# A hybrid diffusion step on one core: the backward recurrence's operands in two tiles with slots of their own, and q's low half over fixed zeros

## The chip, the cores and the metric

The kernel runs on one core of one Trainium2 chip. The metric is the device time of one execution in microseconds (us), as the median of several. The engines are TensorE (PE, with its weight load PEld), VectorE (DVE), ScalarE (ACT), GpSimd (POOL) and SyncE (SP). Nearly all transfers between HBM and the on-chip memory are issued by SP, in program order, on one queue.

## The reference, cut to what matters

One layer of a trunk: 128 context tokens and 2048 latent tokens on a grid 64 wide, 1024 channels, all in float32. After a normalisation one product gives q, k, v for 8 heads of 64 channels, and the two inputs of a recurrence over 512 channels. Each latent token attends to an 8 by 16 neighbourhood and to 128 cached context keys; the recurrence runs forward and backward over the tokens:

```python
s_loc = jnp.einsum('bqhd,bkhd->bhqk', qr, kb).astype(jnp.float32) * ATT_SCALE + bias
...
hf = rg_lru(xc, lru_a[0], lru_wr[0], lru_br[0], lru_wi[0], lru_bi[0], h0[:, 0], False)
hb = rg_lru(xc, lru_a[1], lru_wr[1], lru_br[1], lru_wi[1], lru_bi[1], h0[:, 1], True)
out = (hf + hb).astype(yb.dtype) * jax.nn.gelu(yb)
```

Attention and `out` go side by side through one output projection, then come a gated residual, a second normalisation, a SwiGLU feed-forward part and a last normalisation.

## The kernel before

To keep float32 accuracy on PE, an operand x is split into a high part and a low part (x minus the high part), and a product is made of several products of parts. The kernel runs in phases: 1 makes q, k, v and the forward recurrence and writes them to scratch in HBM (`qs`, `ks`, `vs`, `lrs`); 2 is attention together with the backward recurrence; 3a is the output projection; 4 and 5 are the feed-forward part. The order of instructions is written out by hand and each engine works through its own list in order.

**Phase 2, attention.** Heads go in four pairs p. The latent grid is cut into 16 blocks of 128 queries, four row blocks rb by four column blocks cb; a fifth row block, rb 4, holds the context tokens. So there are 4 times 17 = 68 blocks, and each has one unit for each of the two heads: 136 units. For the unit at hand `scores` multiplies q by the keys on PE (L913 to L917), and DVE adds the bias (L921); one unit later `probs` takes the exponential (ACT, DVE, POOL); four units later the probabilities are transposed and multiplied by v.

**q and k.** A key tile of a head holds the high half of k in partitions 0 to 63 and its low half in 64 to 127 (`load_keys`, four transfers of 576 KB a pair). `load_rows` loads q of a pair and row block so that the high half of q stands in both halves of the partitions, and the low half of q too: one tile [128, 4, 512], filled by four transfers of 256 KB, each into 64 partitions (L841). Two products with 128 rows of contraction then sum all four products of parts. The tiles of row blocks 0 to 3 share three slots; rb 4 has a tile of its own, `qc`. `load_rows` also loads the values `vg`. The loads are issued two row blocks ahead; at the start of rb 1 come the next pair's bias tables `tz`, keys `k` and context values `vc`.

**The backward recurrence.** `backward` walks through 20 pieces: for each of the four channel groups m four pieces of 512 tokens and one of 128, from the end to the start. For a piece one transfer (L765) fills a tile `bk` [128, 4, 512] with the decay a, the input b, the forward result hf and the gate gl; there are three slots. DVE scans a and b (L780), adds b to hf (L785), multiplies by gl (L788), and SP stores hf to `mix` (L89). It is a generator that is resumed at every second unit, once a block: a piece of 512 takes three blocks, one of 128 takes one. The load of piece i + 2 is issued one block after the scan of piece i:

```python
            nc.vector.tensor_copy((self.st[:, 4 + m:5 + m] if s0 == 0 else self.bstate[:, m:m + 1]), b[:, 0:1])
            if s0:
                yield
            load(i + 2)
            nc.vector.tensor_add(hf, hf, b)
```

Its slot is that of piece i - 1, whose last reader is the store of hf. A store is put on a list and issued at the start of the next unit.

**SP.** SP's list holds loads and stores in program order, and an instruction that waits holds all behind it. Each transfer counts up one of eight completion counters, DMAHW0 to DMAHW7 in turn, and waits until the transfer eight places before it has landed; so at most eight are in flight.

Of the kernel before, what the change touches and what calls it, by code (L numbers as in the profile page):

```python
# [6 lines left out]
F32 = mybir.dt.float32  # L7
F32R = mybir.dt.float32r
BF16 = mybir.dt.bfloat16
AF = mybir.ActivationFunctionType  # L10
OP = mybir.AluOpType
# [36 lines left out]
def f32(ap):  # L48
    return ap.bitcast(F32)
# [16 lines left out]
class Body:  # L66
# [687 lines left out]
    def backward(self, bp):  # L754

        nc = self.nc
        seq = [(m, s0, n) for m in range(4)
               for s0, n in ((1664, 512), (1152, 512), (640, 512), (128, 512), (0, 128))]
        T = {}

        def load(i):
            if i < len(seq):
                m, s0, n = seq[i]
                T[i] = bp.tile([128, 4, 512], F32, name="bk", bufs=3)
                nc.sync.dma_start(T[i][:, :, :n], self.lrs[m, :, :, s0:s0 + n])  # L765

        for i in range(2):
            load(i)
            yield
            yield  # L770
        for i, (m, s0, n) in enumerate(seq):
            t = T.pop(i)
            a, b, hf, gl = (t[:, j, :n] for j in range(4))
            if s0 == 0:
                init = 0.0
            elif s0 == 1664:
                init = self.prm[:, P_ST + 4 + m:P_ST + 5 + m]
            else:
                init = self.bstate[:, m:m + 1]
            nc.vector.tensor_tensor_scan(b[:, ::-1], a[:, ::-1], b[:, ::-1], initial=init, op0=OP.mult, op1=OP.add)  # L780
            nc.vector.tensor_copy((self.st[:, 4 + m:5 + m] if s0 == 0 else self.bstate[:, m:m + 1]), b[:, 0:1])
            if s0:
                yield
            load(i + 2)
            nc.vector.tensor_add(hf, hf, b)  # L785
            if s0:
                yield
            nc.vector.tensor_mul(hf, hf, gl)  # L788
            self.store(self.mix[4 + m, :, s0:s0 + n], hf)
            yield  # L790
# [17 lines left out]

    def att_more(self):
        self.te = self.pool("attb", side="right")  # L810
        self.load_rows(0, 0)
        self.load_bias(0)
        self.load_rows(0, 1)
# [18 lines left out]
    def load_rows(self, p, rb):  # L832

        nc, tp = self.nc, self.te
        ctx = rb == 4
        c0, nq = 512 * rb, 128 if ctx else 512
        q = self.Q[p, rb] = tp.tile([128, 4, nq], F32R, name="qc" if ctx else "q", bufs=1 if ctx else 3)
        for h in range(2):
            src = f32(self.qs[p, :, 64 * h:64 * h + 64, c0:c0 + nq]).rearrange("z f n -> f z n")
            for i in range(2):  # L840
                nc.sync.dma_start(f32(q[64 * i:64 * i + 64, 2 * h:2 * h + 2]), src)  # L841
        if not ctx:
            row0, nr = ROWS[rb][:2]
            for G in range(row0 // 4, (row0 + nr) // 4):
                if (p, G) not in self.V:
                    v = self.V[p, G] = tp.tile([128, 4, 128], F32, name="vg", bufs=8)
                    vd = self.vs[:, G, :, 128 * p:128 * p + 128].rearrange("w k d -> k w d")
                    nc.sync.dma_start(v[:, 1:3], vd[:, 1:3])
                    nc.sync.dma_start(v[:96, 0:4:3], vd[:96, 0:4:3])

    def phase2(self):
        nc, A = self.nc, self.A
        self.ps = self.pool("psum2", space=PSUM)
        tp = self.pool("attw", side="right")
        self.wop = self.pool("wo")
        self.wo = {}
        bp = self.pool("bk")
        K, TZ, Q, V, MO, BT = self.K, self.TZ, self.Q, self.V, {}, {}
# [13 lines left out]
        def bias(blk, h):  # L872

            p, rb, cb = blk
            if rb == 4:
                return bts[0]
            row0, nr, I0, rt = ROWS[rb]
            col0, wc, J0, ct = COLS[cb]
            key = (p, rt, ct, h)
            if key not in BT:  # L880
                BT[key] = bts[nbt[0] % 4]
                nbt[0] += 1
                mo = MOFF[rt, ct]
                nc.gpsimd.tensor_add(
                    BT[key][:, 512 - nr * wc:512].rearrange("p (i j) -> p i j", i=nr),
                    TZ[p, h][:, I0:I0 + nr, J0:J0 + wc],
                    msk[:, mo:mo + nr * wc].rearrange("p (i j) -> p i j", i=nr))
            return BT[key]

        def geom(blk):  # L890
            p, rb, cb = blk
            if rb == 4:
                return 512, 0, 128
            nr, wc = ROWS[rb][1], COLS[cb][1]
            return 512 - nr * wc, nr // 4, 4 * wc
# [3 lines left out]
        def scores(u):  # L899
            blk, h = u  # L900
            p, rb, cb = blk
            off = geom(blk)[0]
            bt = bias(blk, h)
            kt = K[p, h]
            qs = slice(128 * cb, 128 * cb + 128)

            q, r = (Q[p, rb][:, 2 * h + z, qs] for z in range(2))
            S = self.b2()
            if off < 512:
                row0, nr = ROWS[rb][:2]  # L910
                col0, wc = COLS[cb][:2]
                kw = kt[:, 0:2048].rearrange("p (r c) -> p r c", c=64)[:, row0:row0 + nr, col0:col0 + wc]
                nc.tensor.matmul(S[:, off:512], q, kw, start=True, stop=False)  # L913
                nc.tensor.matmul(S[:, off:512], r, kw, start=False, stop=True)
            kc = kt[:, 2176:2304] if rb == 4 else kt[:, 2048:2176]
            nc.tensor.matmul(S[:, 512:640], q, kc, start=True, stop=False)
            nc.tensor.matmul(S[:, 512:640], r, kc, start=False, stop=True)  # L917
            P[u] = tp.tile([128, 640], F32, name="pt", bufs=5)
            SM[u] = tp.tile([128, 4], F32, name="sm", bufs=7)

            nc.vector.tensor_tensor_reduce(out=P[u][:, off:640], in0=S[:, off:640], in1=bt[:, off:640],  # L921
                                           scale=-1.0, scalar=3.0e38, op0=OP.add, op1=OP.min,
                                           accum_out=SM[u][:, 0:1])
# [56 lines left out]
        def rest():  # L980
            yield from self.backward(bp)
            nc.sync.dma_start(A["st"], self.st)
            yield
            ks, raw = (4, 5, 6, 7, 0), {}
            for i in range(len(ks) + 1):
                if i < len(ks):
                    raw[i] = bp.tile([128, 4, 512], F32, name="bk", bufs=3)[:, 0:2].rearrange("p a b -> p (a b)")
                    nc.sync.dma_start(raw[i], A["w_out"][128 * ks[i]:128 * ks[i] + 128, :])
                if i:
                    self.split_wo(self.wop, raw.pop(i - 1), ks[i - 1])  # L990
                yield

        rest = rest()
        units = [(b, h) for b in blocks for h in range(2)]
        nu = len(units)
        LA = 4
        done, opened = None, False
        for i in range(nu + LA + 1):
# [4 lines left out]
            if i < nu:  # L1003
                (p, rb, cb), h = units[i]
                if h == 0 and cb == 0:
                    if rb == 0:
                        self.load_rows(p, 2)
                    elif rb == 1:
                        self.load_rows(p, 3)
                        if p < 3:  # L1010
                            self.load_bias(p + 1)
                            self.load_keys(p + 1)
                            self.load_values(p + 1)
                    elif rb == 3:
                        self.load_rows(p, 4)
                        if p < 3:
                            self.load_rows(p + 1, 0)
                    elif rb == 4 and p < 3:
                        self.load_rows(p + 1, 1)
                scores(units[i])  # L1020
# [13 lines left out]
            if i % 2 and not opened:  # L1034
                try:
                    next(rest)
                except StopIteration:
                    bp.release()
                    self.opened()
                    opened = True  # L1040
# [594 lines left out]
```

## Time and profile before

| | us |
|---|---|
| median of 3 runs (2618.84 to 2628.18) | 2619.93 |
| the profiled execution's own time | 2630.12 |
| its span, first to last instruction | 2628.3 |
| PE busy in the span | 2485.7 (95%) |
| DVE, POOL, ACT busy | 1545.8, 1422.5, 991.5 |
| phase 2, about | 638 to 935 us of the span |

A stretch of the trace has the busy time of each engine with the number of its instructions, then three columns: TensorE's granted clock as a share of full speed, the mean busy share of the 16 DMA engines, and GB/s moved. A wait is put down to the instruction that came last. "SPq" is SP's transfer queue; its durations are those of issuing a transfer, not of moving the data. All times in a timeline count from the span's start.

### The profile page before, as it was taken

The numbers are of one execution on the slowest core, as the hardware profiler recorded it, in microseconds if no ns is written. First come the engines' busy times: TensorE is split into PE (matmuls) and PEld (weight loads), VectorE is DVE, ScalarE is ACT, GpSimd is POOL, SyncE is SP. The second block draws the span as 40 slices with busy tenths as digits, with TensorE's granted clock in tenths as the row PEclk, the third lists the DMA queues.
The fourth block names the chain that finished last, engine by engine and source line by source line (L and its number), as shares of the span: only waits on it lengthen the run. The fifth ranks groups of instructions, "written<-read, shape, count | busy, mean of one in ns | idle before, by whom it ended". The sixth has DMA issues, their size and how long they took to land. (4 is left out here: it accounts for less than half of the span.)

```text
span 2628.3 us, 37477 instructions
## 1 busy us (share of the span) xinstructions
PE 2485.7 (95%) x13976; PEld 2205.0 (84%) x13976; DVE 1545.8 (59%) x2252; ACT 991.5 (38%) x1696; POOL 1422.5 (54%) x962
## 2 busy tenths in 40 slices
PE   7899999999887999979999999999999999999998
PEld 4888777787776788869999999999999978888887
DVE  5665757673665743477666887888666721123222
ACT  3454455565554632133333444443333310021111
POOL 3444455554555644467766788888666532233121
PEclk8999999999988999989999999999999999999999
DMA  6455767559988755734333243323332463343331
GB/s 254 136 167 209 261 200 260 183 192 249 233 230 228 187 168 181 234 111 145 105 100 105 81 167 101 119 92 104 99 105 89 138 243 131 112 144 121 127 108 65
DMA packets 234086, 412.88 MB, mean 157 GB/s; under 512 B 33705, under 2 KB 125609, under 8 KB 232881
## 3 DMA queue, kind: packets, MB, share of 16 engines
q1 hardware_dynamic: 233904, 410.49, 49.0%
q8 instruction: 111, 1.82, 0.3%
q14 instruction: 71, 0.57, 0.1%
HBM read 300.17 MB, written 119.69 MB: 160 GB/s over the span
## 5 line engine op out<-in xcount | busy, mean ns | idle before, releaser
L116 POOL TENSOR_TENSOR wl<-wr,wh 128x1024 fp32r<-128x1024 f32 (+1 forms) x146 | 303.5, 2079 | 384.7 <-ACT wh L110 109.5
L116 POOL TENSOR_TENSOR wl<-su,wh 128x512 fp32r<-128x512 f32 x263 | 396.0, 1534 | 30.3 <-ACT wh L110 29.8
L1488 POOL TENSOR_TENSOR x<-x,tm 128x1024 f32<-128x1024 f32 x33 | 100.0, 3032 | 337.6 <-DVE tm L1487 334.6
L110 ACT ACTIVATE wh<-su 128x512 fp32r<-128x512 f32 x263 | 160.4, 628 | 274.9 <-DVE su L1263 133.4
L546 PE MATMUL mm<-hh,wh 128*128 128x512 f32 (+2 forms) x640 | 213.8, 367 | 7.4 <-DVE hh L112 6.5
L546 PE MATMUL mm<-hl,wh 128*128 128x512 f32 (+2 forms) x640 | 212.2, 364 | 4.5 <-DVE hl L116 4.5
L546 PE MATMUL mm<-hh,wl 128*128 128x512 f32 (+2 forms) x640 | 211.2, 363 | 1.1 <-POOL wl L116 1.1
L1487 DVE TENSOR_TENSOR tm<-b,g 128x1024 f32<-128x1024 f32 x33 | 40.4, 1224 | 289.0 <-PE b L1477 277.4
L1359 POOL TENSOR_TENSOR ua<-ua,gt 128x384 f32<-128x384 f32 (+3 forms) x99 | 165.0, 1673 | 57.8 <-DVE ua L1339 44.5
L930 POOL TENSOR_SCALAR pt<-pt,sm 128x512 f32<-128x512 f32 (+3 forms) x136 | 113.0, 831 | 119.3 <-DVE sm L929 94.1
L116 DVE TENSOR_TENSOR wl<-wr,wh 128x512 fp32r<-128x512 f32 x131 | 140.1, 1069 | 57.2 <-ACT wh L110 57.2
L1263 DVE TENSOR_TENSOR su<-wr 128x512 f32<-128x512 f32 x66 | 115.4, 1749 | 74.5 <-POOL wl L116 74.5
L1474 PE MATMUL b<-wdl,b0h 128*128 128x512 f32 x374 | 147.7, 395 | 3.0 <-POOL wdl L116 2.3
L1473 PE MATMUL b<-wdh,b0h 128*128 128x512 f32 x374 | 147.2, 393 | 1.3 <-ACT wdh L110 1.3
L110 ACT ACTIVATE wh<-wr 128x512 fp32r<-128x512 f32 (+1 forms) x198 | 120.6, 622 | 68.1 <-PE pp L1318 61.6
L546 PEld LDWEIGHTS mm<-hh,wh 128*128 128x128 f32 x640 | 114.5, 193 | 29.6 <-ACT hh L110 8.6
L1474 PE MATMUL b<-wdl,b1h 128*128 128x512 f32 x352 | 138.7, 394 | 0.0
L1473 PE MATMUL b<-wdh,b1h 128*128 128x512 f32 x352 | 138.4, 393 | 0.0
L112 DVE CAST wh<-wr 128x1024 fp32r<-128x1024 f32 x79 | 60.5, 767 | 124.2 <-PE mm L546 73.5
L546 PEld LDWEIGHTS mm<-hl,wh 128*128 128x128 f32 x640 | 114.1, 193 | 20.7 <-DVE hl L116 6.0
L928 ACT ACTIVATE pt<-pt,sm 128x512 f32<-128x512 f32 (+3 forms) x136 | 95.8, 704 | 84.9 <-DVE sm L921 67.2
L546 PEld LDWEIGHTS mm<-hh,wl 128*128 128x128 f32 x640 | 113.7, 192 | 16.7 <-POOL wl L116 1.4
(315 smaller groups left out, 7479.0 us busy)
## 6 DMA issues: line engine op xcount, KB each, us to landing
wr<-in_win SPq DMA_DIRECT2D x80, 512.0 KB
wr<-in_wg SPq DMA_DIRECT2D x66, 512.0 KB
wr<-in_wu SPq DMA_DIRECT2D x66, 512.0 KB
ar<-act_s SPq DMA_DIRECT2D x15, 1408.0 KB
wm<-in_w_mod SPq DMA_DIRECT2D x40, 512.0 KB
x_s<-x SPq DMA_DIRECT2D x34, 512.0 KB
x<-x_s SPq DMA_DIRECT2D x34, 512.0 KB
act_s<-ua SPq DMA_DIRECT2D x44, 384.0 KB
```

The costliest lines, as they stand in the source:

```text
L110: self.nc.scalar.activation(hi, src, AF.Copy)
L112: self.nc.vector.tensor_copy(hi, src)
L116: e.tensor_sub(lo, src, f32(hi))
L546: nc.tensor.matmul(p[:, :x1 - x0], a[:, s], b[k][:, x0:x1], start=first, stop=last)
L928: nc.scalar.activation(x, x, AF.Exp, bias=sm[:, 0:1], scale=-1.0, accum_out=sm[:, 1:2])
L930: nc.gpsimd.tensor_scalar(x, x, sm[:, 2:3], 0.0, op0=OP.mult, op1=OP.add)
L1263: nc.vector.tensor_sub(t, a11, a21)
L1359: self.nc.gpsimd.tensor_mul(O[i][:, a:b], O[i][:, a:b], G[i][:, a:b])
L1473: nc.tensor.matmul(ps[:, s], ah[:, i], wh[:, s], start=(i == 0), stop=False)
L1474: nc.tensor.matmul(ps[:, s], ah[:, i], wl[:, s], start=False, stop=False)
L1487: nc.vector.tensor_mul(tmp, ps, g2[1 if t == 0 else 0])
L1488: nc.gpsimd.tensor_add(x2, x2, tmp)
```

## The change

**Backward recurrence.** The tile `bk` becomes two: `bk0` [128, 2, 512] for a and b with three slots, and `bk2` [128, 2, 512] for hf and gl with four. A piece is loaded by two transfers of 512 KB in place of one of 1 MB. The load of piece i + 2 is issued ahead of the scan of piece i, one block earlier than before. Its a and b take the slot of piece i - 1 (last reader: the add on DVE), its hf and gl that of piece i - 2 (last reader: that piece's store).

**q.** The high half stays in both halves of the partitions, in a tile `q` [128, 2, 512] with three slots, which rb 4 now shares. The low half goes into one of three fixed tiles `ql` [128, 2, 512], in partitions 0 to 63 alone; partitions 64 to 127 hold zeros, written once by GpSimd at the end of phase 1. The product of the two low halves drops out. A row block's q is three transfers of 256 KB in place of four. PE's instructions keep their number and shapes.

```diff
-                T[i] = bp.tile([128, 4, 512], F32, name="bk", bufs=3)
-                nc.sync.dma_start(T[i][:, :, :n], self.lrs[m, :, :, s0:s0 + n])
+                T[i] = []
+                for j, bufs in ((0, 3), (2, 4)):
+                    t = bp.tile([128, 2, 512], F32, name=f"bk{j}", bufs=bufs)
+                    nc.sync.dma_start(t[:, :, :n], self.lrs[m, :, j:j + 2, s0:s0 + n])
+                    T[i] += [t[:, 0, :n], t[:, 1, :n]]
...
-            t = T.pop(i)
-            a, b, hf, gl = (t[:, j, :n] for j in range(4))
+            a, b, hf, gl = T.pop(i)
+            load(i + 2)
...
             if s0:
                 yield
-            load(i + 2)
             nc.vector.tensor_add(hf, hf, b)
...
         self.te = self.pool("attb", side="right")
+
+        self.ql, self.nql = [self.te.tile([128, 2, 512], F32R, name=f"ql{i}") for i in range(3)], 0
+        for t in self.ql:
+            self.nc.gpsimd.tensor_scalar(t[64:128].rearrange("p a b -> p (a b)"),
+                                         self.ident[64:128, 0:1].to_broadcast([64, 1024]), 0.0, 0.0,
+                                         op0=OP.mult, op1=OP.add)
...
-        q = self.Q[p, rb] = tp.tile([128, 4, nq], F32R, name="qc" if ctx else "q", bufs=1 if ctx else 3)
-        for h in range(2):
-            src = f32(self.qs[p, :, 64 * h:64 * h + 64, c0:c0 + nq]).rearrange("z f n -> f z n")
-            for i in range(2):
-                nc.sync.dma_start(f32(q[64 * i:64 * i + 64, 2 * h:2 * h + 2]), src)
+        q = tp.tile([128, 2, 512], F32R, name="q", bufs=3)[:, :, :nq]
+        r = self.ql[self.nql % 3][:, :, :nq]
+        self.nql += 1
+        self.Q[p, rb] = q, r
+        for z, d in ((0, q[0:64]), (0, q[64:128]), (1, r[0:64])):
+            nc.sync.dma_start(f32(d), f32(self.qs[p, z, :, c0:c0 + nq]).rearrange("(h f) n -> f h n", f=64))
...
-            q, r = (Q[p, rb][:, 2 * h + z, qs] for z in range(2))
+            q, r = (z[:, h, qs] for z in Q[p, rb])
...
-                    raw[i] = bp.tile([128, 4, 512], F32, name="bk", bufs=3)[:, 0:2].rearrange("p a b -> p (a b)")
+                    raw[i] = bp.tile([128, 2, 512], F32, name="bk2", bufs=4).rearrange("p a b -> p (a b)")
```

SP's list where the second pair turns to its row block 1 (the third pair's `tz`, `k0`, `k1` and `vc` are loaded here; the `bk` load is that of piece 8), before:

```order
L841 DMA q_6676<-qs_s_62 64x2x512 x4
L848 DMA vg_6681<-vs_s_65 128x2x128
L849 DMA vg_6681<-vs_s_65 96x2x128
L824 DMA tz_6684<-tz_s_73 128x512
L824 DMA tz_6686<-tz_s_73 128x512
L830 DMA k0_6688<-ks_s_63 64x2304 x2
L830 DMA k1_6691<-ks_s_63 64x2304 x2
L819 DMA vc_6694<-in_cv 128x128
L819 DMA vc_6694<-vctx_s_66 128x128
L765 DMA bk_6743<-lrs_s_67 128x4x512
```

The same place of the list with the change:

```order
L768 DMA bk0_6688<-lrs_s_67 128x2x512
L768 DMA bk2_6690<-lrs_s_67 128x2x512
L851 DMA q_6694<-qs_s_62 64x2x512 x2
L851 DMA ql2_5407<-qs_s_62 64x2x512
L858 DMA vg_6698<-vs_s_65 128x2x128
L859 DMA vg_6698<-vs_s_65 96x2x128
L833 DMA tz_6701<-tz_s_73 128x512
L833 DMA tz_6703<-tz_s_73 128x512
L839 DMA k0_6705<-ks_s_63 64x2304 x2
L839 DMA k1_6708<-ks_s_63 64x2304 x2
L828 DMA vc_6711<-in_cv 128x128
```

The load of piece 8 moved from behind q, the bias tables and the keys to ahead of them, and q has one transfer fewer.

SP's list at the same turn one pair later, with what each transfer waits for (a counter DMAHW is that of an earlier transfer); `bk_7823` is piece 15, and `mix_s_68<-bk_7333` stores piece 12, whose slot it takes, before:

```order
L819 DMA vc_7667<-in_cv 128x128 [waits DMAHW3_49]
L819 DMA vc_7667<-vctx_s_66 128x128 [waits DMAHW4_49]
L89 DMA mix_s_68<-bk_7333 128x512 [waits DMAHW5_49,DVE_49]
L89 DMA mix_s_68<-mo_7625 128x512 [waits DMAHW6_49,DVE_49]
L765 DMA bk_7823<-lrs_s_67 128x4x512 [waits DMAHW7_49,DMAHW5_49]
L89 DMA mix_s_68<-bk_7503 128x512 [waits DMAHW0_49,DVE_49]
```

And with the change, where piece 15 is `bk0_7790` and `bk2_7792`:

```order
L828 DMA vc_7689<-in_cv 128x128 [waits DMAHW4_49]
L828 DMA vc_7689<-vctx_s_66 128x128 [waits DMAHW5_49]
L89 DMA mix_s_68<-bk2_7299 128x512 [waits DMAHW6_49,DVE_49]
L768 DMA bk0_7790<-lrs_s_67 128x2x512 [waits DMAHW7_49]
L768 DMA bk2_7792<-lrs_s_67 128x2x512 [waits DMAHW0_49]
L89 DMA mix_s_68<-mo_7650 128x512 [waits DMAHW1_49,DVE_49]
L89 DMA mix_s_68<-bk2_7462 128x512 [waits DMAHW2_49,DVE_49]
```

The load of piece 15 stands behind the keys in both, but the second wait, for the store of piece 12 that was issued two places ahead of it (DMAHW5), is gone.

GpSimd's list at the end of phase 1 with the change; the `wl` are the low halves of phase 1's last three weight tiles, and `bt0` is phase 2's first bias tile:

```order
L709 TENSOR_TENSOR ig_5268<-ig_5268,xc_5080 128x514
L116 TENSOR_TENSOR wl_5320<-wr_5239,wh_5319 128x1024
L116 TENSOR_TENSOR wl_5361<-wr_5276,wh_5360 128x1024
L817 TENSOR_SCALAR ql0_5405<-ident_76 64x1024
L817 TENSOR_SCALAR ql1_5406<-ident_76 64x1024
L817 TENSOR_SCALAR ql2_5407<-ident_76 64x1024
L116 TENSOR_TENSOR wl_5439<-wr_5323,wh_5438 128x1024
L894 TENSOR_TENSOR bt0_5551<-tz_5424,msk_4542 128x288
```

The three fills are new; they stand ahead of the last weight tile's low half.

## Rows read from the trace of the kernel before

**Rows 1.** The profiled execution, its span.

```profile
core 0: 2628.3 us, clock 0.975
```

**Rows 2.** Busy time by stretch: phase 2; 20 us without a wait.

```profile
core 0: us, PE busy (x) PEld busy (x) DVE busy (x) ACT busy (x) POOL busy (x), PEclk, DMA share, GB/s
640.00:935.00 295.00, 243.91 (x2257) 211.59 (x2259) 195.99 (x660) 168.29 (x410) 174.18 (x207) 0.90 0.84 222
850.00:870.00 20.00, 20.00 (x214) 17.84 (x211) 16.31 (x59) 13.93 (x38) 17.66 (x21) 1.00 0.91 222
```

**Rows 3.** Waits of PE and DVE, 636 to 935 us: total, times, longest (us).

```profile
PE b L913 <- DVE sm L921: 47.0, 13, 14.5
DVE bk L780 <- DMA bk<-lrs_s: 42.8, 9, 15.2
...
PE b L913 <- DMA q<-qs_s: 3.7, 2, 2.3
```

**Rows 4.** Timeline of DVE, three scans, one restart; in brackets: idle before.

```profile
714.44 1.28 DVE L780 TENSOR_TENSOR_SCAN bk<-bk,prm 128x512 f32<-128x512 f32 x1 [5.46 <-DMA bk<-lrs_s]
...
757.88 1.28 DVE L780 TENSOR_TENSOR_SCAN bk<-bk,bstate 128x512 f32<-128x512 f32 x1 [10.43 <-DMA bk<-lrs_s]
...
764.90 0.29 DVE L974 COPY mo<-b 128x128 f32<-128x128 f32 x1 [2.07 <-PE b L966]
...
839.47 1.28 DVE L780 TENSOR_TENSOR_SCAN bk<-bk,prm 128x512 f32<-128x512 f32 x1 [15.22 <-DMA bk<-lrs_s]
```

**Rows 5.** Waits of SP's transfer queue, 620 to 935 us.

```profile
SPq L765 <- DMA mix_s<-bk: 56.7, 10, 9.3
...
SPq L89 <- DMA q<-qs_s: 9.5, 15, 1.2
...
SPq L841 <- PE b L966: 2.7, 4, 1.1
```

**Rows 6.** Timeline of SP's transfer queue: start, duration of the issue (us).

```profile
708.53 0.56 SPq L765 DMA_DIRECT2D bk<-lrs_s  x1
...
729.81 2.58 SPq L841 DMA_DIRECT2D q<-qs_s  x4
...
737.90 3.63 SPq L830 DMA_DIRECT2D k<-ks_s  x4
...
742.92 0.57 SPq L765 DMA_DIRECT2D bk<-lrs_s  x1
...
820.86 0.32 SPq L89 DMA_DIRECT2D mix_s<-bk  x1
...
833.65 0.58 SPq L765 DMA_DIRECT2D bk<-lrs_s  x1
```

**Rows 7.** Busy time by stretch: keys alone in flight; 128-partition transfers.

```profile
747.00:754.00 7.00, 3.40 (x37) 2.83 (x35) 0.45 (x4) 1.65 (x4) 1.68 (x2) 0.88 1.01 214
921.00:925.00 4.00, 4.00 (x46) 3.49 (x41) 2.92 (x14) 3.25 (x9) 3.00 (x6) 1.00 1.06 398
```

**Rows 8.** SP's issue of three 512 KB loads; size and count of q's loads.

```profile
918.64 1.54 SPq L1057 DMA_DIRECT2D x<-in_w_out  x3
...
q<-qs_s SPq DMA_DIRECT2D x64, 256.0 KB
```

**Rows 9.** GpSimd around phase 1's end, its nearest shape, PE in the last block.

```profile
623.22 2.39 POOL L116 TENSOR_TENSOR wl<-wr,wh 128x1024 fp32r<-128x1024 f32 x1 [1.94 <-DVE wh L112]
638.71 1.42 POOL L884 TENSOR_TENSOR bt<-tz,msk 128x288 f32<-128x288 f32 x2 [13.11 <-PE mm L546]
...
L930 POOL TENSOR_SCALAR pt<-pt,sm 128x640 f32<-128x640 f32 x32 | 30.8, 963 | 53.4 <-DVE sm L929 38.6 <-PE b L917 5.6 <-DVE mo L974 5.0
...
637.28 0.39 PE L546 MATMUL mm<-hh,wh 128*128 128x512 f32 x1
637.51 0.39 PE L546 MATMUL mm<-hl,wh 128*128 128x512 f32 x1
```

## The prediction

> **What bounds the kernel now.** The change touches phase 2 and one spot at the end of phase 1, so I first read the stretch of phase 2 by itself [rows 2]. PE is busy for 243.9 of 295 us there, at a mean granted clock of 0.90 (1.00 is the higher level, 2.4 GHz). In 20 us without a stall (850 to 870) PE is busy all the time at clock 1.00 and does 214 of the stretch's 2257 matmuls, that is 6.4 of the 68 blocks: 3.1 us a block. At that pace the stretch would take 211 us; so up to 84 us of it are waits and what they bring. The transfer engines, too, are busy: 0.84 of the stretch, and 0.91 in the 20 us in which PE did not wait.
>
> The waits say whose they are [rows 3]. PE's largest, 47.0 us, is for DVE's bias step (L921). DVE is not slow there: its own largest wait is the backward scan's for its operands, 42.8 us in nine times, the longest 15.2. DVE works in order, so the bias steps behind the scan wait with it, and PE behind them. PE waits for q itself only 3.7 us. The timeline has the three large scan waits: 5.46, 10.43 and 15.22 us [rows 4]; the other six share the remaining 11.7. After the 10.43 the pipeline also has to fill again: DVE stands 2.07 us for PE 6 us later.
>
> Why are the operands late? SP's own waits [rows 5] give 56.7 us to the load of `bk` waiting for the store of an earlier piece, whose slot it takes; SP is held that long, and so is every load and store behind. The timeline of the queue [rows 6] shows two kinds. At 742.92 the load is issued right behind four key transfers (737.90) and the scan starts 15 us later: it stands in line. At 820.86 the store is issued, again behind keys, and only at 833.65 does the load follow it: it waits for the store's landing, and the scan starts at 839.47.
>
> How fast is the line? With keys alone in flight, which go into 64 partitions, it moves 214 GB/s with all engines busy; with loads into 128 partitions 398 GB/s [rows 7]. A transfer of q, 256 KB into 64 partitions, thus takes 1.22 us, a key transfer 2.76 and half a `bk` tile 1.32. The Trainium skill ("SBUF — State Buffer", "Door 1: The DMA port swizzle") says that partitions 0 to 63 reach 8 of 16 ports, half of the bandwidth; the trace agrees, 214 to 398.
>
> **The change, part by part.**
>
> *Piece 8.* Its load moves ahead of q, the bias tables and the keys, where q stood at 729.81 [rows 6]: 13.1 us earlier, which is more than the wait of 10.43. Saved 10.4, and the refill of 2.1 behind it [rows 4].
>
> *Piece 5.* Its load at 708.53 had waited for a store; it now needs none that is recent and goes a block (3.1 us) earlier, with half a tile ahead of the scan instead of a whole one (1.3 less). Saved 5.5; at least 3.
>
> *Piece 15.* Its load stays behind the keys but no longer waits for the store's landing at 833.6. It lies right behind that store in the line: half a tile later, 834.9, less one q transfer that is no longer ahead, 833.7. The scan started at 839.47. Saved 5.8, and 9.4 of the wait stay; 3 to 15 as bounds.
>
> *The other six waits, 11.7 us.* Each load goes a block earlier, has half a tile less (1.3) and mostly a q transfer less (1.2) before the scan can start; the mean wait is 2.0. I take 10 as saved, bounds 7 and 11.7.
>
> *What is late next.* Without the pause at piece 8 the scans of pieces 9 and 10 come while the keys (four at 2.76, 11 us) still move, and their loads stand behind these; piece 10's hf and gl also wait for a store that lies behind the keys. I take 2 us of new waits, between 0 and 5.
>
> *q's transfers.* One of four goes [rows 8]. Of the 16 loads of 1 MB three lie at or before the start of phase 2; 13 transfers at 1.22 and four small ones at 0.31 are 17 us of transfer time. They shorten the line, and what of that reaches a scan is counted above; it isn't added again. As a check: 0.84 of 295 us are 248 us of transfer time, 231 after; in a phase of 263 us that is 0.88, below the 0.91 that the line reached while PE never waited. So the line can carry the forecast.
>
> *SP.* q loses 20 issues, `bk` gains 20; an issue takes 0.56 to 0.65 us [rows 6]. Nothing, as SP's queue has waits to spare once the 56.7 are gone.
>
> *The fills.* Three GpSimd operations of 64 by 1024 ahead of the last weight tile's low half. The nearest row, 128 by 640, takes 963 ns [rows 9], hence 1.5 us each. GpSimd is free from 621.3 (1.94 us idle before 623.22); three fills end at 625.9, the low half at 628.3 instead of 625.6. Its block is the last of phase 1: 24 matmuls 0.23 us apart that end at 638.6, so it starts at about 633.1. Hidden, with 4.8 us of cover; a fill would have to take over 3.1 us to cost anything. PE's products with the zero rows keep their shapes: nothing.
>
> *Sum.* 10.4 + 2.1 + 5.5 + 5.8 + 10 - 2 = 31.8 us. The profiled execution took 2630.1 us, its span 2628.3 [rows 1] and 1.8 around it; it becomes 2598. It lies above all three timed runs, whose median is 2619.9; the same saving there gives 2588. With all low bounds (10.4 + 3 + 3 + 7 - 5, no refill) 18 us are saved, with all high ones (42.8 and two refills) 47: from 2573 to 2602.
>
> **The rivals.** *The line is the bound (2603).* The transfer engines are busy 0.84 of the phase already, and an earlier load only stands longer in it. Then the gain is the transfer time cut, 17 us. For it: at 742.92 the load did stand in line, and stores wait for q transfers, with which they share nothing but the counter [rows 5]. Against it: the 0.88 above.
>
> *Halves cost as much as wholes (2620).* Alone, a load of 1 MB took 5.9 us (708.53 to the scan at 714.44), against 2.6 at 398 GB/s: 3.3 us fixed. If each of the 20 added transfers paid that in the line, 66 us would go; from 1.6 on the gain is used up. Against it: three loads of 512 KB issued within 1.54 us [rows 8] ran at 398 GB/s together [rows 7]. The pieces were loaded two ahead before as well, so that the change might do little is part of this case. The Trainium skill ("DMA: Bandwidth & Descriptors", "Measured") asks for transfers of at least 1 MiB, and its section "Anatomy of one DMA" puts a fixed cost of about 2.0 us on each, measured on GpSimd's path; by that, 20 more would cost an estimated 40 us in the line and the time would be 2628. The 398 GB/s speak against it for transfers in a row.
>
> *The shared ring holds SP (2635, slower).* With rb 4 in q's ring, the first three row blocks of pairs 1 to 3 take a slot that PE has only just left, where before it had been left a block or more earlier: nine loads at which SP may stand for PE, with all stores and `bk` loads behind. To end above 2633 each must keep the line idle for over 5.0 us ((31.8 + 13.1) / 9); at 5.2 the time is 2635. Against it: today's waits of this kind are 2.7 us in four [rows 5], PE needs q ten units (five blocks, 15 us) after the issue, and SP is late rather than early.
>
> **How the numbers follow.** What a measurement can tell here is about 0.5%, 13.1 us. Chances: forecast 0.76; the line 0.13, of which 0.03 would stay within 0.5%; halves 0.07; the ring 0.04. Faster: 0.76 + 0.10 = 0.86; same 0.10; slower 0.04. The range takes in the forecast's bounds but for the last 3 us of the high ones, and the line's 2603 with 3 us to spare: 2576 to 2606.
>
> **What would show it.** DVE's wait at the scan falls from 42.8 to about 13 us, nearly all of it at piece 15; the wait at piece 8 is gone; SP's wait of the `bk` load for a store falls from 56.7 to under 20; phase 2 takes about 263 us with a transfer share of 0.88; phase 1 ends at the same time. I am wrong if DVE still waits over 25 us there, if PE's wait for q grows to over 10, or if the transfer share reaches 1.0 while scans wait at every piece.

## The result and the profile after

The changed kernel takes 2581.7 us (median of four runs, 2573.7 to 2584.1) against 2621.3 for the kernel before (2618.8 to 2628.2 in four): the ratio is 0.984, 95% interval 0.981 to 0.987. That is faster by 39.6 us, or 1.5%. The profiled execution took 2581.9 us, its span 2580.1.

Phase 2 from its first bias step to its last, in the columns of [rows 2]; the first row is of the kernel before, the second of the changed one:

```profile
639.50:931.30 291.80, 240.60 (x2227) 209.07 (x2226) 194.51 (x654) 165.34 (x403) 173.90 (x205) 0.90 0.85 225
636.20:883.30 247.10, 231.90 (x2227) 201.84 (x2227) 195.02 (x654) 165.93 (x403) 179.20 (x204) 0.97 0.93 248
```

The phase is 44.7 us shorter, 247.1 in place of 291.8. PE does 2227 matmuls in both. Its idle time falls from 51.2 to 15.2 us, 36.0 less; the other 8.7 us are that it is busy for a shorter time with as many matmuls, at a mean granted clock of 0.97 in place of 0.90. What comes behind takes 1697.0 and 1696.8 us.

The waits of PE and of DVE after, 636 to 900 us:

```profile
PE b L923 <- DVE sm L931: 11.1, 14, 3.2
PE b L923 <- DMA q<-qs_s: 2.9, 1, 2.9
PE b L924 <- DMA ql<-qs_s: 1.0, 1, 1.0
```

```profile
DVE bk L784 <- DMA bk<-lrs_s: 6.1, 3, 4.2
```

These answer to [rows 3]: the scan's wait for its operands fell from 42.8 to 6.1 us, and PE's wait for the bias step from 47.0 to 11.1. Where the 6.1 are, and what came of piece 8, the scans in DVE's timeline show (start, duration, and in brackets the idle time before):

```profile
678.61 1.28 DVE L784 TENSOR_TENSOR_SCAN bk<-bk,bstate 128x512 f32<-128x512 f32 x1 [4.18 <-DMA bk<-lrs_s]
...
733.65 1.27 DVE L784 TENSOR_TENSOR_SCAN bk<-bk,bstate 128x512 f32<-128x512 f32 x1
744.11 0.41 DVE L784 TENSOR_TENSOR_SCAN bk<-bk 128x128 f32<-128x128 f32 x1
747.86 1.27 DVE L784 TENSOR_TENSOR_SCAN bk<-bk,prm 128x512 f32<-128x512 f32 x1
757.05 1.83 DVE L784 TENSOR_TENSOR_SCAN bk<-bk,bstate 128x512 f32<-128x512 f32 x1 [0.67 <-DMA bk<-lrs_s]
...
800.56 1.73 DVE L784 TENSOR_TENSOR_SCAN bk<-bk,prm 128x512 f32<-128x512 f32 x1 [1.20 <-DMA bk<-lrs_s]
```

The rows are pieces 2, 8, 9, 10, 11 and 15 (counted from 0). Pieces 8, 9 and 10 wait for nothing; of the 15.22 us at piece 15 [rows 4] 1.20 are left. The longest wait is now at piece 2, which stands behind the keys of the second pair; it was 3.15 us before and has grown.

SP's waits, 620 to 900 us, answer to [rows 5]:

```profile
SPq L89 <- DVE mo L984: 20.9, 8, 10.8
SPq L768 <- DMA k<-ks_s: 16.2, 7, 2.8
...
SPq L851 <- PE b L950: 8.9, 1, 8.9
SPq L768 <- DMA mix_s<-bk: 6.2, 5, 2.4
```

The `bk` load's wait for a store fell from 56.7 to 6.2 us. What holds that load most now are the keys ahead of it in the line, 16.2 us. The 20.9 us are stores that wait for DVE's results, 19.4 of them after 840 us, when no `bk` load is left to come.

GpSimd around the end of phase 1, with the three fills:

```profile
615.64 2.40 POOL L116 TENSOR_TENSOR wl<-wr,wh 128x1024 fp32r<-128x1024 f32 x1 [3.92 <-issue]
618.13 3.65 POOL L817 TENSOR_SCALAR ql<-ident 64x1024 fp32r<-64x1024 f32 x3
621.86 2.40 POOL L116 TENSOR_TENSOR wl<-wr,wh 128x1024 fp32r<-128x1024 f32 x1
```

They take 3.65 us together and stand behind a low half that ends at 618.0; the last low half ends at 624.3, before the 625.6 of [rows 9].

The span fell by 48.2 us, more than the median, because the one profiled execution of the kernel before lies 8.8 us above its median and that of the changed kernel at its own. 3.3 of the 48.2 are the earlier end of phase 1, which lies between 635.5 and 639.5 us in the thirteen profiles of this study, with and without the change.

### The profile page after: what moved, and what is told of

Its sections match the earlier page's. It is cut to its first block, busy times and chain, and to the rows that moved or that the text cites. A ratio compares the mean times of both kernels' runs of the same rounds, so it can differ in the third digit from the quotient of the medians.

```text
span 2580.1 us, 37465 instructions
## 1 busy us (share of the span) xinstructions
PE 2474.4 (96%) x13976; PEld 2195.5 (85%) x13976; DVE 1545.4 (60%) x2252; ACT 992.0 (38%) x1696; POOL 1432.5 (56%) x965
## 5 line engine op out<-in xcount | busy, mean ns | idle before, releaser
L1487 PE MATMUL b<-wdh,b0l 128*128 128x512 f32 x374 | 116.6, 393 | 0.0
```

Source lines behind the costliest of these rows:

```text
L1487: nc.tensor.matmul(ps[:, s], al[:, i], wh[:, s], start=False, stop=(i == 10))
```

## The experiments

Unless a diff says otherwise it is against the changed kernel. Scan waits, SP waits and the length of phase 2 (first bias step to last) are of each kernel's one profile, times are medians. The kernel before was timed again beside them, with medians of 2621.1 to 2623.2 us.

**The two parts apart.** First q's part alone, with `bk` as before; then `bk`'s part alone, with q as before.

```diff
 q alone
-                T[i] = []
-                for j, bufs in ((0, 3), (2, 4)):
...
+                T[i] = bp.tile([128, 4, 512], F32, name="bk", bufs=3)
+                nc.sync.dma_start(T[i][:, :, :n], self.lrs[m, :, :, s0:s0 + n])
...
-            load(i + 2)
...
             if s0:
                 yield
+            load(i + 2)
```

> Only q's part of the change (three transfers for four, shared ring, zero fills); the backward recurrence is that of before. Theory A (the operands come late because SP is held for a store's landing and the load stands behind the keys): those holds stay, each scan gains at most the q transfers no longer ahead of it, so 8 to 16 us are saved (2605 to 2613) and DVE's wait at the scan stays above 25 us, with SP's wait of the bk load for a store above 35 us. Theory B (the line's transfer time is the cause): most of the whole gain of 40 us is here, below 2596, and DVE's wait at the scan falls below 15 us.

Measured: 2607.1 us (ratio 0.994, 0.993 to 0.996), 14.9 below the kernel before timed beside it (2622.0). The waits of the scan and of SP:

```profile
DVE bk L781 <- DMA bk<-lrs_s: 28.7, 7, 14.5
```

```profile
SPq L766 <- DMA mix_s<-bk: 61.9, 12, 11.4
```

```diff
 bk alone
-        q = tp.tile([128, 2, 512], F32R, name="q", bufs=3)[:, :, :nq]
-        r = self.ql[self.nql % 3][:, :, :nq]
...
+        q = self.Q[p, rb] = tp.tile([128, 4, nq], F32R, name="qc" if ctx else "q", bufs=1 if ctx else 3)
...
+                nc.sync.dma_start(f32(q[64 * i:64 * i + 64, 2 * h:2 * h + 2]), src)
```

> Only the backward recurrence's part (two tiles with three and four slots, loaded a block earlier); q is loaded as before. Theory A: 20 to 28 us saved (2593 to 2601), SP's wait of the bk load for a store falls below 12 us, the wait at piece 8 is gone, those at pieces 2 and 15 stay in part. Theory B: under 10 us saved, since the same bytes stand in the line, with DVE's wait at the scan above 30 us.

Measured: 2599.0 us (0.991, 0.988 to 0.993), 23.0 below. Here SP is free and the line is longer:

```profile
DVE bk L783 <- DMA bk<-lrs_s: 19.4, 5, 5.6
```

```profile
SPq L767 <- DMA mix_s<-bk: 5.7, 4, 2.7
```

So 14.9 us come from q's part and 23.0 from that of `bk`; together 37.9, against 39.6 for both: the parts add, as far as their intervals tell. Theory A held in both. q's part leaves the hold as it is (61.9) and piece 15's wait with it (14.5); `bk`'s part removes the hold but its scans wait behind the longer line at five pieces.

**What in the `bk` part does it.** Four kernels: the change with the late load; one early load of 1 MB into one tile with three slots; the change with three slots for hf and gl; the one tile with four slots.

```diff
 late load
             a, b, hf, gl = T.pop(i)
-            load(i + 2)
...
             if s0:
                 yield
+            load(i + 2)
```

> The change with the load at its old place, one block after the scan; two tiles with slots of their own stay. Theory A (slots count most, place only where it moves past the keys): the wait at piece 8 comes back with 5 to 9 us, the rest stays as in the changed kernel: 5 to 9 us slower than it, 2587 to 2591. Rival (the early place is what counts): most of the gain is lost, above 2600.

Measured: 2594.5 us (0.989, 0.988 to 0.991), 12.8 above the change: more than the 5 to 9 of theory A, and short of the rival's 2600. Piece 8 waits again (7.4 us), and so does piece 15 (7.9), although SP's wait for a store is only 9.4: the earlier request alone is worth this.

```diff
 one tile, early load
-                for j, bufs in ((0, 3), (2, 4)):
...
+                T[i] = bp.tile([128, 4, 512], F32, name="bk", bufs=3)
```

> The change, but a, b, hf and gl in one tile of three slots again, one transfer of 1 MB, still issued a block earlier (ahead of the scan). Theory A: the load now waits for a store that was only just issued, SP is held longer than before the change, and the early place gains nothing: between q alone and 4 us worse than it, 2605 to 2617; SP's wait of the bk load for a store is above 50 us. Rival (the early place is what counts, the slots do not): within 6 us of the changed kernel, 2582 to 2588.

Measured: 2612.8 us (0.996, 0.994 to 0.997). SP's wait for stores grew to 76.6 us in 14 times: a load asked for earlier into a slot that isn't free holds the queue longer. The scan still waits 29.6 us.

```diff
 three slots
-                for j, bufs in ((0, 3), (2, 4)):
+                for j, bufs in ((0, 3), (2, 3)):
```

> The changed kernel, but hf and gl have three slots instead of four, so their load waits again for the store of the piece just ended. Theory A (the hold of SP by that store is the largest cause): SP's wait of the bk load for a store is above 45 us again, and the time is 18 to 30 us above the changed kernel's, 2600 to 2612. Rival (two tiles and the early place are enough): within 6 us of it, below 2588.

Measured: 2600.0 us (0.991, 0.989 to 0.993), 18.3 above the change for one slot less. SP's waits and PE's in this kernel:

```profile
SPq L768 <- DMA mix_s<-bk: 53.8, 13, 12.0
```

```profile
PE b L923 <- DMA q<-qs_s: 6.5, 2, 4.0
PE b L924 <- DMA ql<-qs_s: 2.6, 4, 1.0
```

The scan waits for 13.0 us here, 6.9 more than with the change; its a and b have a slot that no store holds. SP's hold also delays q, behind the held load: PE waits 9.1 us for it, against 3.9 with the change.

```diff
 one tile, four slots, early load
-                for j, bufs in ((0, 3), (2, 4)):
...
+                T[i] = bp.tile([128, 4, 512], F32, name="bk", bufs=4)
```

> The changed kernel, but a, b, hf and gl in one tile of 1 MB with four slots, loaded by one transfer at the early place. Theory A: SP is not held (its wait of the load for a store stays below 15 us); a scan waits for the whole tile, 1.3 us more at the few pieces that still wait: 0 to 6 us above the changed kernel, 2582 to 2588. Rival (the half that comes first counts most): more than 15 us above it, over 2597.

Measured: 2590.4 us (0.988, 0.986 to 0.990), a little above the range expected, and SP's wait for stores is 18.1 us where under 15 was expected. Against the one tile with three slots (2612.8) the fourth slot is worth 22.4 us; against this kernel the two tiles of the change are worth 8.7 more, with 28 KB in a partition in place of 32. With 18.1 us of such waits, not all of the 8.7 need be the half tile less ahead of the scan.

**Do smaller transfers cost?** Each tile of the change is filled by two transfers of 256 KB in place of one of 512 KB, 40 transfers more.

```diff
-                    nc.sync.dma_start(t[:, :, :n], self.lrs[m, :, j:j + 2, s0:s0 + n])
+                    for z in range(2):
+                        nc.sync.dma_start(t[:, z, :n], self.lrs[m, :, j + z, s0:s0 + n])
```

> The changed kernel with a piece loaded by four transfers of 256 KB instead of two of 512 KB, same slots, same place: 40 transfers more. Theory A (in the line a transfer costs its bytes, 0.66 us each at 398 GB/s; only the eight counters fill sooner): 0 to 8 us above the changed kernel, 2582 to 2590. Rival (a fixed cost a transfer in the line, the case of halves that cost as much as wholes): 1.6 us or more each, 64 us, above 2640.

Measured: 2583.7 us (0.986, 0.983 to 0.989; 2581.3 to 2595.0), which is not to be told from the change. In the profile there is a cost: phase 2 is 4.9 us longer (252.0 against 247.1), some 0.12 us for each transfer more, and the scan waits 14.2 us in place of 6.1:

```profile
DVE bk L785 <- DMA bk<-lrs_s: 14.2, 3, 5.2
```

**Is what is left the line?** The keys are the largest transfers of phase 2 into 64 partitions. Here the scratch for them is laid out so that one transfer of 1152 KB fills all 128 partitions of a key tile; phase 1 stores them in twice as many transfers of half the size.

```diff
-                self.store(f32(self.ks[m, z, :, col:col + n]), f32(t))
+            for i in range(2):
+                s = slice(64 * i, 64 * i + 64)
+                self.store(f32(self.ks[m, i, 64 * z:64 * z + 64, col:col + n]), f32(t[s]))
...
-            for z in range(2):
-                self.nc.sync.dma_start(f32(k[64 * z:64 * z + 64]), f32(self.ks[p, z, 64 * h:64 * h + 64]))
+            self.nc.sync.dma_start(f32(k), f32(self.ks[p, h]))
```

> The changed kernel with the keys' scratch laid out so that a key tile is one transfer of 1.15 MB into 128 partitions instead of two of 576 KB into 64 each; phase 1 stores them by twice as many transfers of half the size. Theory A (what is left are loads behind the keys): a tile takes 2.9 us in the line instead of 5.5, so 5 us less at each of three turns; the waits at pieces 2 and 15 and the wait for q go, with what they bring: 6 to 15 us below the changed kernel, 2567 to 2576. Rival (phase 2 is bound by PE and DVE now): within 4 us of it, above 2577.

Measured: 2571.9 us (0.981, 0.978 to 0.983; 2569.5 to 2575.0), 9.8 below the change. By stretch, first with a key tile in flight, then phase 2; and the scan's one wait:

```profile
729.00:734.00 5.00, 5.00 (x49) 4.30 (x50) 4.12 (x15) 3.94 (x8) 3.45 (x4) 1.00 1.00 389
```

```profile
640.00:890.00 250.00, 237.91 (x2297) 206.30 (x2296) 199.97 (x662) 172.97 (x415) 184.61 (x206) 0.98 0.87 252
```

```profile
DVE bk L786 <- DMA bk<-lrs_s: 2.1, 1, 2.1
```

The line moves 389 GB/s there, in place of the 214 of [rows 7]; at that rate a key tile is 3.0 us long in place of two times 2.76. From the first bias step to the last phase 2 takes 239.2 us, 7.9 less than with the change.

In the next kernel the keys are as in the change, but the next pair's `tz`, keys and `vc` are requested two blocks later, so that the loads of pieces 2, 8 and 15 stand ahead of them:

```diff
+                if (h, cb, rb) == (0, 1, 1) and p < 3:
+                    self.load_bias(p + 1)
+                    self.load_keys(p + 1)
+                    self.load_values(p + 1)
...
-                        if p < 3:
-                            self.load_bias(p + 1)
-                            self.load_keys(p + 1)
-                            self.load_values(p + 1)
```

> The change, with the next pair's key and value tiles requested two blocks later (after the loads of backward pieces 2, 8 and 15, instead of ahead of them). A (what is left of the scan's waits is the load's place behind the keys in SP's list): the waits at pieces 2 and 15 (4.2 and 1.2 us) go, the line's bytes are the same, and the time is 2572 to 2579 us. B (the bytes, not their order): the waits move to other pieces or to q, their sum stays above 4 us and the time is within 4 us of the change's 2581.7. C (keys too late): TensorE waits for keys at a pair's start and the time is above 2586 us.

Measured: 2581.5 us (0.984, 0.983 to 0.986): no gain. PE's waits, and the scan's:

```profile
PE b L923 <- DMA q<-qs_s: 6.1, 2, 3.2
PE b L924 <- DMA ql<-qs_s: 1.1, 2, 0.7
```

```profile
DVE bk L784 <- DMA bk<-lrs_s: 0.7, 2, 0.5
```

B holds: the scan's waits are gone (0.7), and PE waits 7.2 us for q in place of 3.9. What stood behind the keys was exchanged, the bytes were not.

Both together, keys in one transfer and later (the two diffs above):

> The change with keys as one 128-partition transfer for each tile, and requested two blocks later as well. A (with the keys at 128 partitions the line is no longer what phase 2 waits for): the order is worth nothing more, the time is within 4 us of the 2571.9 us of the run with 128-partition keys alone. B (the line is still what holds it): more than 5 us below that, under 2567 us.

Measured: 2573.6 us (0.981, 0.980 to 0.983): the same as with 128-partition keys alone, so A. It also shows their gain a second time.

And the kernel before, with the 128-partition keys as its only change:

> The kernel before, with its bk tile, two slots and late load as they were, and keys alone as one 128-partition transfer for each tile. A (the held loads of bk and the line are two causes): the line is shorter, SP's wait of a bk load for a store stays above 35 us, the scan still waits for 20 to 35 us in sum, and the time is 2603 to 2612 us. B (the keys in the line were the main cause of the scan's waits): under 2595 us and less than 15 us of scan waits. C (half-rate keys cost nothing while the loads are held): above 2616 us.

Measured: 2608.8 us (0.994, 0.992 to 0.997), 14.4 below the kernel before; the scan waits 22.9 us and the load's wait for a store is unchanged:

```profile
DVE bk L782 <- DMA bk<-lrs_s: 22.9, 7, 9.4
```

```profile
SPq L767 <- DMA mix_s<-bk: 56.3, 10, 9.8
```

A holds: a shorter line helps without touching the hold, as q's part alone did.

## Why the prediction was right, point by point

The mechanism and the sign were right and the time lies in the range, 6.3 us below the value forecast: 31.8 us were forecast and 39.6 came (the median before is 1.4 higher with its fourth run). The sum was made from the profile, though, and there the phase is 44.7 us shorter, 12.9 more than forecast; that the times lie closer is in part luck, as the profiled execution before was 8.8 us above its median. By terms, with the phase of the two profiles:

| term | forecast | between the two profiles |
|---|---|---|
| piece 8 | 10.4 | 10.4 |
| piece 5 | 5.5 | 5.5 |
| piece 15 | 5.8 | 14.0 |
| the other six waits | 10 | 6.9 |
| new waits at pieces 9 and 10 | -2 | 0 |
| refill | 2.1 | 8.0 as the rest of the 44.7, mostly PE's own pace |

*Pieces 8 and 5* went as forecast; the late load brings 7.4 us of wait back at piece 8, so it was the place in the list. At piece 5 more than one thing would have done: with q's part alone, the load's slot and place as before, 1.0 us of the 5.46 is left, and with the late load none.

*Piece 15 is the term that was mis-sized.* I counted only the hold of its own load. From the first of the key transfers ahead of it to the scan it was 24.2 us before, to 839.47; the first row is of SP's timeline before, the two others of that after:

```profile
815.28 4.20 SPq L830 DMA_DIRECT2D k<-ks_s  x4
```

```profile
781.87 2.80 SPq L839 DMA_DIRECT2D k<-ks_s  x4
...
786.72 3.51 SPq L768 DMA_DIRECT2D bk<-lrs_s  x2
```

After it is 18.7 us, from 781.87 to 800.56. That is 5.5 less, as the 5.8 said. But both of the other ends moved too. The table counts from the start of the scan of piece 12, which waits for nothing in any of these kernels (794.46 us before, 766.61 after). A wait is the second column and the third together, less the fourth:

| us | first key transfer goes out | from there to the scan of piece 15 | DVE ready for it | wait | PE's waits for q in between |
|---|---|---|---|---|---|
| before | 20.8 | 24.2 | 29.8 | 15.2 | 2.3 |
| the change | 15.3 | 18.7 | 32.8 | 1.2 | 3.9 |
| q's part alone | 17.6 | 23.9 | 27.1 | 14.5 | 1.0 |
| `bk`'s part alone | 18.8 | 19.2 | 32.4 | 5.6 | 5.2 |
| late load | 15.0 | 19.8 | 26.9 | 7.9 | 1.3 |

So the 14.0 us are 5.5 for the load's own way, 5.6 because SP's list, keys included, was earlier, and 3.0 because DVE came later. The first belongs to `bk`'s part, as forecast (5.0 with it alone, 0.3 with q's). To the second both parts give something (3.2 with q's alone, 2.0 with `bk`'s), so it is not the hold alone that had made the list late. The third is no gain. In the change PE stands for q between pieces 12 and 13, and DVE behind it for 3.69 us (at 777.88):

```profile
775.45 0.41 PE L923 MATMUL b<-k,q 128*128 128x384 f32 x1 [2.89 <-DMA q<-qs_s]
```

With the late load PE hardly stands there and DVE is ready 5.9 us earlier, with the keys as early as in the change: that is most of the 7.9 us that it waits at piece 15. With 128-partition keys PE's wait for q there is 0.7 us and the scan of piece 15 waits for nothing.

*The other six waits* were taken together at 10 of 11.7. Piece 2 has 4.18 us, where it had 3.15, and piece 11 has 0.67. Piece 2 stands behind keys as piece 8 did, and the prediction did not ask where in the list its load goes. With the keys later the wait goes, and with 128-partition keys it goes too.

*New waits* did not come: pieces 9 and 10 start without one.

*The refill* was the wrong term. It counted the time in which DVE starts again after a stall, once, at piece 8. PE's idle time fell by 36.0 us, about the 36.7 by which the scan's waits fell, so that next to nothing is left for starting again. What the sum left out is that PE itself took 8.7 us less for the same 2227 matmuls, at a mean granted clock of 0.97 in place of 0.90.

*q's transfers.* That their 17 us must not be added to the scan's waits was right; q's part alone is worth 14.9.

*The fills* take 1.22 us each, where 1.5 was estimated, and are hidden. *SP's issues* cost nothing that shows.

*The signs to look for.* The scan's wait was to be about 13 us, nearly all at piece 15: it is 6.1, most of it at piece 2. SP's wait for stores was to be under 20: 6.2. The phase was to take about 263 us of the 295 with a share of 0.88: it takes some 250 (295 less 44.7). The share between the bias steps is 0.93 of 247.1 us, or 230 us of transfer time, as the 231 of the forecast, in a shorter phase; it is above the 0.91 that the forecast took for what the line had reached.

**The rivals.** *The line is the bound* fell as a forecast of 2603, but names what is left: with the hold gone, changing the order gains nothing (keys later, 2581.5), and fewer microseconds in the line gain 9.8 (128-partition keys, 2571.9). *Halves cost as much as wholes* fell: with quarters the phase is 4.9 us longer, and the time is not to be told from the change. By the Trainium skill ("DMA: Bandwidth & Descriptors", "Anatomy of one DMA"), whose 2.0 us are of GpSimd's path, 40 more transfers would be an estimated 80 us. The profile shows 4.9 us, so for transfers in a row that cost does not add up. *The shared ring* fell: at L851 SP stands for PE once for 8.9 us, before 860.8 us, when the last scan (839.34) is over, and otherwise 7.8 us in seventeen short waits, not 5.0 at each of nine loads. For `bk`'s own slots that rival's mechanism is real: with three slots for hf and gl SP's hold comes back (53.8 us) and 18.3 us with it, partly as PE's wait for q.

**What stays open.** The phase is 44.7 us shorter and phase 1 ended 3.3 earlier between the two profiles, while the medians differ by 39.6. So about 9 us of the profiled execution before are its own, and the terms above may hold some of it. Why PE waits longer for q between pieces 12 and 13 with the change than before (3.9 and 2.3 us) was not tested by itself; the 128-partition keys remove most of it. How much of PE's 8.7 us the clock alone is, no run took apart.

## What to carry to other kernels

When a queue works in order, look for the load that waits for a store: it delays everything behind it. Price a late operand from a fixed point ahead of it: when its list goes out, how long its own way takes, and when its reader is ready. Here all three moved, and only the second had been forecast. A slot more for the operand with the late last reader, and a tile of its own for it, costs less than a bigger ring for all: here the split with 28 KB beat one tile with 32 KB by 8.7 us. Here, with the hold gone, a new order of the loads gained nothing and a shorter line did: a transfer that fills all 128 partitions was worth a new layout of the scratch, 9.8 us.

## What the runs showed of the hardware

- Transfers of 256 KB in a row cost their bytes and little more: with 40 more of them phase 2 was 4.9 us longer, the median 2.0, which is within the spread.
- With transfers of 1152 KB into 128 partitions in flight the line moved 389 GB/s, where keys into 64 partitions at a time moved at 214 GB/s [rows 7], with all engines busy in both. The prediction had the rate but not its worth: 9.8 us in a kernel where PE is busy for 96% of the span.
- PE took 240.6 us for 2227 matmuls in a phase with 51.2 us of idle time and a mean granted clock of 0.90, and 231.9 us for as many with 15.2 us of idle time and 0.97.
- A GpSimd fill of 64 by 1024 took 1.22 us and the 128 by 640 operation 0.963 [rows 9]: 1.19 and 1.50 ns for each element of a partition.
